# Two hybrid decoder layers: wider spacing in the gate chain, a second output tile, key and query stores and attention one step later

## The chip, the cores and the metric

The kernel runs on one core of one Trainium2 chip. Its engines work side by side, each through its own list of instructions in order: TensorE (PE, matrix products; PEld are its weight loads), VectorE (DVE), ScalarE (ACT), GpSimd (POOL) and SyncE (SP, which issues most of the DMAs). An instruction that needs another engine's result waits on a semaphore, and everything behind it on its engine waits too. The metric is the device time of one execution in microseconds (us), lower is better; the times are medians of a few runs.

## What is computed

Two layers over 1024 positions of width 1024. Each layer has an adaptive norm, one wide projection, four mLSTM heads and four retention heads of width 256, an output projection and a gated residual. Cut to what matters here:

```python
for l in range(2):
    shift, scale, gate = split(silu(c) @ w_ada[l] + b_ada[l], 3)
    h = rmsnorm(x, norm_g[l]) * (1 + scale) + shift
    mq, mk, mv, mo, mz, mi, mf, rq, rk, rv, rz = split_cols(h @ w_in[l])
    mq, mk = split(silu(causal_conv4(concat(mq, mk)) + conv_b))
    cell = mlstm(mq, mk, mv, mi + b_i, mf + b_f)   # exp input gate, sigmoid forget gate, running max
    y_m = sigmoid(mo) * head_norm(cell) * silu(mz)
    ret = retention(rotary(rq), rotary(rk), rv)    # decay 1 - 2^(-5-head)
    y_r = head_norm(ret) * silu(rz)
    x = x + gate * (concat(y_m, y_r) @ w_out[l])
return rmsnorm(x, final_g)
```

The mLSTM needs, per head and position, running sums of the log forget gate and a running maximum of the input gate minus that sum. That small computation on 4 heads x 1024 positions is the *gate chain* below. All matrix products run in pairs of rounded parts (high and low), three products for one (`mm3`, lines 177 to 179).

## The kernel before

**Products.** The projections of a layer are a list of jobs (`plan`): `v45` the values of heads 4 and 5, `z4` the gate path of head 4, `q4` and `k4` its queries and keys, `a..` gate paths of mLSTM heads. Heads 0 to 3 are mLSTM, 4 to 7 retention. In layer 0 the list starts `v45 v67 z4 q4 k4 z5 q5 k5`, in layer 1 `v45 z4 q4 k4 q5 k5 v67`. A job is one level of a seven-product scheme: products a11, S1, S2, a12, S4, S3, a22 over half-size operands, each 12 matmuls of 512 columns, or for values twice 24 matmuls of 256 columns. One such product is a *step*. Products collect in four PSUM banks, px and pz, two of each; ScalarE (L775, L825, L830) and VectorE (L778, L782, L785, L826, L832, L835) move them out to tiles `acc`, a pool of 12. Weights come as tiles R by DMA; ScalarE rounds them to wH (L404) and VectorE or GpSimd makes the low part (L409).

**What sets the order.** TensorE's order is the order of the code. After every step `tick()` runs whatever small generators are due: a generator's `yield n` puts its next part off by n steps. So the number of products between two parts of a generator is the number in its `yield`. On the other engines a list scheduler places the instructions by its own estimate, apart from those marked `late(...)`, which keep the program's order. On VectorE, `Later()` marks whole helpers so (their records all have line L144).

**The gate chain** (`gate_chain`, L502 to L597) is such a generator. Parts: raw gates from PSUM to SBUF on ScalarE; store to DRAM and load back with 32 partitions of 128 positions; log sigmoid on ScalarE; on VectorE the two running sums (`bq`, `br`); then TensorE sums the carries over blocks (L547), VectorE adds them and takes the running maximum; TensorE transposes the block maxima (L556); VectorE scans them; TensorE spreads the result (L561); VectorE finishes; store of the maximum to DRAM (L567); TensorE transposes four tables (L571) and VectorE and ScalarE make the factors for the mLSTM. In layer 0 it runs beside `rotary_tables`, and in both layers beside `build_forms`, which makes half-size sums of the inputs on VectorE (L634 to L655).

**Keys and queries.** `conv_chain` (mLSTM) and `rot_done.chain` (retention) end in `spill`: the tile is stored to DRAM (qdr or kfr, L935), and for keys a VectorE transpose of it (L902) is stored too (kdr, L904). All go through SP's queue.

**Attention** of a head (`attention`) starts 4 steps after its key job has ended and follows `TABLE`, one entry for each step: loads of q, k, v from DRAM (L999, L1013), splits (L876, L928, L929), scores S, values V, state updates U (L1099, L1102, L1104). `values` collects the output of one chunk of 256 positions in a tile: `nd` for mLSTM (one buffer, 258 columns per half with the denominator), `n` for retention (one buffer). `normalise` and `finish` read it later and transpose it (L1192) before the store (L1197). The only other user of `nd` is a rotary table, which holds it from its load (L975, L976) to the last retention key.

The yields of the chain, in order, are

```python
yield 3   # before the load back
yield 3   # before the log sigmoid
yield 2   # before the running sums
yield 3   # before L547
yield 3   # before L556
yield 3   # before L561
```

Of the kernel before, what the change touches and what calls it, by code (L numbers as in the profile page):

```python
# [19 lines left out]
P = 128  # L20
# [67 lines left out]
def tile_hybrid_trunk(ctx, tc, x, xt, c, positions, w_ada, b_ada, norm_g, w_in, w_blk, w_val, conv_w, conv_b,  # L88
# [415 lines left out]
    def gate_chain(l, pgs, gt):  # L504
# [5 lines left out]
        for half in range(2):  # L510
            for r in (0, 32):
                A.activation(raw[r:r + 4, half * HALF:(half + 1) * HALF], pgs[half][r:r + 4, :], AF.Identity,
                             bias=bg[r:r + 4, :])
        for i in range(2):
            Q.dma_start(gtd[l][i], raw[32 * i:32 * i + 4, :])
# [13 lines left out]
        yield 3  # L529
        for i, t in enumerate((fb, li)):  # L530
            Q.dma_start(t, gtd[l][i].rearrange("h (b t) -> (h b) t", t=P))
        yield 3
# [3 lines left out]
        yield 2  # L536
# [7 lines left out]
        yield 3  # L544
# [9 lines left out]
        yield 3  # L554
# [4 lines left out]
        yield 3  # L559
# [319 lines left out]
    def conv_chain(l, hg, which, m, half, pt):  # L879
# [16 lines left out]
        spill(acc, l, hg, which, m, half)  # L896

    def k_store(src, l, hg, m, half):
        zt = wt("acc", 512, NACC)
        n = HALF - half * CH  # L900
        a = n // P
        V.transpose(zt[:, 0:n].rearrange("p (b a c) -> p a b c", a=a, c=32),  # L902
                    src[:, 0:n].rearrange("p (a b c) -> p a b c", a=a, c=32))
        late(Q.dma_start(kdr[l][hg][half][m * P:(m + 1) * P, 0:n], zt[:, 0:n]))  # L904
# [26 lines left out]
    def spill(src, l, hg, which, m, half):  # L931
        dst = (kfr if which else qdr)[l][hg][half].rearrange("(a p) t -> a p t", p=P)
        if which:
            k_store(src, l, hg, m, half)
        late(Q.dma_start(dst[m], src))  # L935
# [16 lines left out]
    def rot_done(l, hg, which, cosT, sinT):  # L952
        got = {}

        def chain(half):
            p0, n1 = got[0, half], got[1, half]
            for m, (one, two, op) in enumerate(((cosT, sinT, ALU.add), (sinT, cosT, ALU.subtract))):
                s, a = wt("acc", 512, NACC), wt("acc", 512, NACC)
                V.tensor_tensor(a, n1, two[half], ALU.mult)
                V.tensor_tensor(s, p0, one[half], ALU.mult)  # L960
                V.tensor_tensor(s, s, a, op)
                yield 1
                spill(s, l, hg, which, m, half)
# [7 lines left out]
    def load_rotary(rot):  # L971
        for which in range(2):
            for i in range(2):
                t = wt("dm", 512, 2) if which == 0 else wt("nd", 516, 1) if i == 0 else bt()
# [10 lines left out]
    def attention(l, hg, gt):  # L985
# [120 lines left out]
        def values(j, tts):  # L1106
            state = st["state"]
            sH, sL = sds[j]
            if tts[0] == 0:
                st["nd"] = wt("nd", 516, 1).rearrange("p (a b) -> p a b", a=2) if ml else None  # L1110
                nrm[j] = st["nd"][:, :, 0:HD] if ml else wt("n", 512, 1).rearrange("p (a b) -> p a b", a=2)
# [358 lines left out]
    for l in range(DEPTH):  # L1470
# [168 lines left out]
        for j, n, part in slots:  # L1639
# [12 lines left out]
            if left[j] == 0 and jobs[j][0] == "k":  # L1652
                launch(attention(l, jobs[j][1][0], gt), 4, 1)
# [67 lines left out]
```

## Time and profile before

| | us |
|---|---|
| median of 3 runs | 2235.43 |
| lowest, highest | 2228.78, 2241.55 |
| profiled execution | 2231.53 |
| its span, first to last instruction | 2229.8 |
| TensorE busy | 2133.3 (96%) |
| VectorE busy | 1779.0 (80%) |
| ScalarE busy | 1144.5 (51%) |
| GpSimd busy | 942.2 (42%) |
| mean granted TensorE clock | 0.991 |

A row of a profile view names line, engine, operation, the tile written and the tile read (`<-`), count, and times. "Idle before, releaser" says what the engine waited for last. PEclk in the table of windows is the share of full clock that TensorE was granted. Matmuls are pipelined: the time of a row is from its start to its modelled end, so the pace of matmuls is read from how many stand in a window.

### The profile page before, as it was taken

The page shows a single profiled execution, that of the slowest core. Times are in us where ns is not written, and L with a number is a line of the kernel's source. Part 1 is how long each engine was busy: PE and PEld are TensorE (multiplying, and loading weights), DVE is VectorE, ACT ScalarE, POOL GpSimd, SP SyncE. Part 2 cuts the span into 40 slices and gives each one's busy share as a digit, 9 for nine tenths or more (in the row PEclk, how much of TensorE's full clock was granted, in tenths as well). Part 3 has the DMA queues.
Part 4 walks back from the last instruction along what each step waited for, and adds up shares of the span by engine and source line. Part 5 has one row for each costly group of instructions (what it writes and reads, how often), then busy time and mean ns, then how long its engine had stood idle before and what let it go on. Part 6 is the DMA issues. An engine that isn't in the chain of part 4 may idle for free.

```text
span 2229.8 us, 35055 instructions
## 1 busy us (share of the span) xinstructions
PE 2133.3 (96%) x11489; PEld 1818.7 (82%) x11489; DVE 1779.0 (80%) x3139; ACT 1144.5 (51%) x2151; POOL 942.2 (42%) x820
## 2 busy tenths in 40 slices
PE   6889999999999999999998999999999899999998
PEld 5688789888988878888777888888987887888887
DVE  6898888999989999874639687788787888978563
ACT  7535345445556656653544434454556555555342
POOL 1433344444454444424466344444434444442313
PEclk9999999999999999999999999999999999999999
DMA  8267678787786667686632866877867677677874
GB/s 290 58 179 214 198 219 258 212 250 210 215 237 184 196 177 208 190 270 221 208 107 68 247 191 189 230 201 221 224 182 194 187 202 194 176 199 247 224 249 119
DMA packets 452836, 448.44 MB, mean 201 GB/s; under 512 B 191314, under 2 KB 310042, under 8 KB 452652
## 3 DMA queue, kind: packets, MB, share of 16 engines
q1 hardware_dynamic: 432924, 410.27, 59.3%
q0 software_dynamic: 19584, 35.66, 10.5%
q8 instruction: 90, 1.47, 0.3%
q14 instruction: 94, 0.77, 0.1%
q10 hardware_dynamic: 144, 0.26, 0.0%
HBM read 322.76 MB, written 123.31 MB: 200 GB/s over the span
## 4 chain that ended last, share of the span: by engine, by line
PE 44%; DVE 27%; DMA 14%; issue 7%; ACT 3%; POOL 2%; SPq 2%; DVEq 0%; POOLq 0%; ACTq 0%
PE px L177 5%; PE px L178 5%; PE px L179 5%; PE pz L178 4%; PE pz L179 4%; PE pz L177 4%; PE pa L177 3%; PE pa L179 3%; PE pa L178 3%; DVE acc L889 3%; DVE R L409 3%; DMA acc<-kfr 2%; DMA R<-in_w_blk_dram 2%; DVE R L713 2%; DMA R<-in_w_val_dram 2%
## 5 line engine op out<-in xcount | busy, mean ns | idle before, releaser
L404 ACT CAST wH<-R 128x512 fp32r<-128x512 f32 x616 | 378.0, 617 | 468.6 <-PE px L178 133.4
L409 POOL TENSOR_TENSOR R<-R,wH 128x512 fp32r<-128x512 f32 x276 | 391.4, 1425 | 483.5 <-ACT wH L404 317.0
L177 PE MATMUL px<-b,wH 128*128 128x512 f32 x912 | 360.7, 395 | 6.4 <-ACT acc L775 5.8
L179 PE MATMUL px<-b,R 128*128 128x512 f32 x912 | 362.1, 397 | 0.0
L178 PE MATMUL px<-b,wH 128*128 128x512 f32 x912 | 360.8, 396 | 0.0
L409 DVE TENSOR_TENSOR R<-R,wH 128x512 fp32r<-128x512 f32 x340 | 261.9, 774 | 97.7 <-ACT wH L404 87.7
L178 PE MATMUL pz<-b,wH 128*128 128x512 f32 x704 | 279.3, 397 | 1.4 <-DVE b L1266 1.4
L179 PE MATMUL pz<-b,R 128*128 128x512 f32 x704 | 280.0, 398 | 0.0
L177 PE MATMUL pz<-b,wH 128*128 128x512 f32 x704 | 279.2, 397 | 0.0
L177 PEld LDWEIGHTS px<-b,wH 128*128 128x128 f32 x912 | 172.2, 189 | 45.4 <-ACT acc L775 7.6
L179 PEld LDWEIGHTS px<-b,R 128*128 128x128 f32 x912 | 171.6, 188 | 40.3
L178 PEld LDWEIGHTS px<-b,wH 128*128 128x128 f32 x912 | 171.9, 188 | 38.6
L177 PE MATMUL px<-wH,b 128*128 128x256 f32 (+1 forms) x576 | 176.9, 307 | 15.9 <-ACT acc L825 5.8
L178 PE MATMUL px<-R,b 128*128 128x256 f32 (+1 forms) x576 | 173.8, 302 | 7.8 <-DVE R L409 7.8
L179 PE MATMUL px<-wH,b 128*128 128x256 f32 (+1 forms) x576 | 174.4, 303 | 0.0
L709 POOL DMA_DIRECT2D R<-in_w_blk_dram x104 | 93.1, 895 | 172.9 <-DMA R<-in_w_blk_dram 61.3
L178 PEld LDWEIGHTS pz<-b,wH 128*128 128x128 f32 x704 | 133.2, 189 | 32.0 <-DVE b L1266 2.3
L179 PEld LDWEIGHTS pz<-b,R 128*128 128x128 f32 x704 | 132.8, 189 | 31.3
L177 PEld LDWEIGHTS pz<-b,wH 128*128 128x128 f32 x704 | 133.2, 189 | 28.5 <-issue 0.2
L877 POOL TENSOR_TENSOR kc<-acc,kc 128x512 fp32r<-128x512 f32 x64 | 88.0, 1375 | 114.2 <-ACT kc L876 109.0
L177 PE MATMUL pz<-wH,b 128*128 128x256 f32 (+1 forms) x448 | 134.1, 299 | 0.3 <-DVE acc L785 0.3
L179 PE MATMUL pz<-wH,b 128*128 128x256 f32 (+1 forms) x448 | 133.8, 299 | 0.0
(345 smaller groups left out, 5282.3 us busy)
## 6 DMA issues: line engine op xcount, KB each, us to landing
R<-in_w_blk_dram SPq DMA_DIRECT2D x276, 256.0 KB
vdr<-acc SPq DMA_DIRECT2D x128, 256.0 KB
ring<-vdr SPq DMA_DIRECT2D x64, 512.0 KB
R<-in_w_out_dram SPq DMA_DIRECT2D x128, 256.0 KB
R<-in_w_blk_dram POOLq DMA_DIRECT2D x104, 256.0 KB, 4.6
R<-in_w_val_dram SPq DMA_DIRECT2D x80, 256.0 KB
gdr<-acc SPq DMA_DIRECT2D x64, 256.0 KB
acc<-in_w_ada_dram SPq DMA_DIRECT2D x64, 256.0 KB
```

Source lines behind the costliest of these rows:

```text
L177: PE.matmul(o, lt[0], rt[0], start=start, stop=False, skip_group_check=more)
L178: PE.matmul(o, lt[0], rt[1], start=False, stop=False, skip_group_check=more)
L179: PE.matmul(o, lt[1], rt[0], start=False, stop=stop, skip_group_check=more)
L404: A.copy(h, r)
L409: eng.tensor_tensor(lo, r, f(h), ALU.subtract)
L709: G.dma_start(raw[n], src, accum_op=ALU.add)
L713: V.tensor_tensor(raw[n], raw[one], raw[two], ALU.add)
L877: eng.tensor_tensor(dst[1], src, f(dst[0]), ALU.subtract)
L889: V.scalar_tensor_tensor(acc[:, e:], pt[:, o + e - d:o + HALF - d], wcol, acc[:, e:], ALU.mult, ALU.add)
```

## The change

Four edits.

1. The gate chain waits longer between its parts: a new `yield 2` between raw gates and their store; then 3, 3, 2, 3, 3, 3 become 4, 4, 3, 6, 5, 5. Its last two yields (2 and 2) stay.
2. `nd` has two buffers, and retention outputs use it too in place of `n`. The rotary table that takes an `nd` keeps one of the two until the last retention key.
3. `spill` becomes a generator: the transpose of a key tile is made as before, the stores to DRAM (kdr, kfr, qdr) are issued one step later.
4. Attention of a head starts 5 steps after its key job instead of 4.

```diff
@@ gate_chain
                              bias=bg[r:r + 4, :])
+        yield 2
         for i in range(2):
             Q.dma_start(gtd[l][i], raw[32 * i:32 * i + 4, :])
...
-        yield 3
+        yield 4
         for i, t in enumerate((fb, li)):
             Q.dma_start(t, gtd[l][i].rearrange("h (b t) -> (h b) t", t=P))
-        yield 3
+        yield 4
         A.activation(e, fb, AF.Abs)
...
-        yield 2
+        yield 3
         V.scalar_tensor_tensor(fb, fb, 0.0, e, ALU.min, ALU.subtract)
...
-        yield 3
+        yield 6
         pc = ps_a()
...
-        yield 3
+        yield 5
         pm = ps_a()
...
-        yield 3
+        yield 5
         pb = ps_a()
@@ conv_chain
-        spill(acc, l, hg, which, m, half)
+        yield from spill(acc, l, hg, which, m, half)
@@ k_store
-        late(Q.dma_start(kdr[l][hg][half][m * P:(m + 1) * P, 0:n], zt[:, 0:n]))
+        return lambda: late(Q.dma_start(kdr[l][hg][half][m * P:(m + 1) * P, 0:n], zt[:, 0:n]))
@@ spill
+        store = k_store(src, l, hg, m, half) if which else None
+        yield 1
         if which:
-            k_store(src, l, hg, m, half)
+            store()
         late(Q.dma_start(dst[m], src))
@@ rot_done
-                spill(s, l, hg, which, m, half)
+                done = spill(s, l, hg, which, m, half)
+                launch(done, next(done))
@@ load_rotary
-                t = wt("dm", 512, 2) if which == 0 else wt("nd", 516, 1) if i == 0 else bt()
+                t = wt("dm", 512, 2) if which == 0 else wt("nd", 516, 2) if i == 0 else bt()
@@ values
-                st["nd"] = wt("nd", 516, 1).rearrange("p (a b) -> p a b", a=2) if ml else None
-                nrm[j] = st["nd"][:, :, 0:HD] if ml else wt("n", 512, 1).rearrange("p (a b) -> p a b", a=2)
+                st["nd"] = wt("nd", 516, 2).rearrange("p (a b) -> p a b", a=2) if ml else None
+                nrm[j] = st["nd"][:, :, 0:HD] if ml else wt("nd", 516, 2)[:, 0:512].rearrange("p (a b) -> p a b", a=2)
@@ the loop over products
-                launch(attention(l, jobs[j][1][0], gt), 4, 1)
+                launch(attention(l, jobs[j][1][0], gt), 5, 1)
```

In the built programs the lines of the changed kernel stand one to four higher than those before.

**The gate chain in layer 1, TensorE.** The carry sums are the two matmuls into a tile `pa` from `q`. Before:

```order
L178 MATMUL pz_13946<-R_13818,b_13584 128x256
L179 MATMUL pz_13946<-wH_13816,b_13585 128x256
L547 MATMUL pa_13973<-q_13547 32x1 x2
L177 MATMUL px_13725<-wH_13907,b_13441 128x256
L178 MATMUL px_13725<-R_13909,b_13441 128x256
```

Now:

```order
L178 MATMUL pz_14229<-b_13575,wH_14124 128x512
L179 MATMUL pz_14229<-b_13574,R_14159 128x512
L548 MATMUL pa_14244<-q_13598 32x1 x2
L177 MATMUL px_14205<-b_13432,wH_14161 128x512
L178 MATMUL px_14205<-b_13433,wH_14161 128x512
```

They have moved from the middle of the value products (256 columns) to behind the first two products of `z4` (512 columns): 144 matmuls of 256 columns and 24 of 512 stand between the old place and the new.

**The same place on VectorE.** The running sums are the SCALAR_TENSOR_TENSOR rows that read `ones`; COPY takes the carries out of `pa`. Before:

```order
L655 SCALAR_TENSOR_TENSOR acc_13895<-acc_13893,acc_13895 128x512
L310 SCALAR_TENSOR_TENSOR acc_13712<-acc_13809,cact,acc_13712 128x512
L144 TENSOR_TENSOR q_13547<-q_13547 32x128
L144 SCALAR_TENSOR_TENSOR q_13547<-ones,q_13547 32x128 x2
L144 TENSOR_SCALAR q_13548<-q_13548 32x128
L144 TENSOR_TENSOR q_13547<-q_13548 32x128
L144 COPY q_13548<-pa_13973 32x2
```

Now, from the second running sum on:

```order
L144 SCALAR_TENSOR_TENSOR q_13598<-ones,q_13598 32x128
L144 TENSOR_SCALAR q_13599<-q_13599 32x128
L144 TENSOR_TENSOR q_13598<-q_13599 32x128
L310 SCALAR_TENSOR_TENSOR acc_13710<-acc_13967,cact,acc_13710 128x512
L310 SCALAR_TENSOR_TENSOR acc_13710<-acc_14044,cact,acc_13710 128x512
L801 SCALAR_TENSOR_TENSOR acc_14080<-px_13723,acc_14079 128x512
L409 TENSOR_TENSOR R_14163<-R_13977,wH_14161 128x512
L836 TENSOR_TENSOR acc_13841<-pz_13905,acc_13841 128x512
L714 TENSOR_TENSOR R_13977<-R_13977,R_14085 128x512
L801 SCALAR_TENSOR_TENSOR acc_14114<-px_13765,acc_14113 128x512
L836 TENSOR_TENSOR acc_13881<-pz_13939,acc_13881 128x512
```

Before, two short rows stood between sums and COPY; now thirteen long ones do, the moves of the last value products out of PSUM among them (COPY is five rows further on).

**ScalarE in layer 0, where the second rotary tables are loaded.** ACT_TABLE_LOAD switches the set of functions; L843 (L844 now) are tanh, L976 (L980 now) sine. Before:

```order
L843 ACT_TABLE_LOAD
L843 ACTIVATE acc_2601<-pz_2586 128x512
L404 CAST wH_2674<-R_2504 128x512
L976 ACT_TABLE_LOAD
L976 ACTIVATE b_2668<-b_2668 128x512
L843 ACT_TABLE_LOAD
L843 ACTIVATE acc_2631<-acc_2574 128x512
L976 ACT_TABLE_LOAD
L976 ACTIVATE dm_2662<-dm_2662 128x512
L404 CAST wH_2697<-R_2611 128x512
L843 ACT_TABLE_LOAD
L843 ACTIVATE acc_2653<-acc_2547 128x512
```

Now:

```order
L844 ACTIVATE acc_2601<-pz_2586 128x512
L404 CAST wH_2674<-R_2481 128x512
L844 ACTIVATE acc_2631<-acc_2574 128x512
L404 CAST wH_2697<-R_2611 128x512
L980 ACT_TABLE_LOAD
L980 ACTIVATE b_2668<-b_2668 128x512
L844 ACT_TABLE_LOAD
L844 ACTIVATE acc_2653<-acc_2524 128x512
L980 ACT_TABLE_LOAD
L980 ACTIVATE dm_2662<-dm_2662 128x512
L404 CAST wH_2723<-R_2481 128x512
L776 COPY acc_2693<-px_2680 128x512
```

Before, five switches stood ahead of the copy of px (L775, one CAST behind the last row shown); now three do, since the exponentials of the chain's end, which share the set of tanh, have moved ahead of this place.

**SP's queue in layer 1, at the key stores of head 5.** L999 (L1003 now) are attention's loads for head 4. Before:

```order
L904 DMA kdr_5_1_214<-acc_15161 128x256
L935 DMA kfr_5_1_278<-acc_15139 128x512
L913 DMA acc_15246<-kdr_4_0_211 32x8x64 x4
L904 DMA kdr_5_1_214<-acc_15219 128x256
L935 DMA kfr_5_1_278<-acc_15165 128x512
L904 DMA kdr_5_0_213<-acc_15223 128x512
L935 DMA kfr_5_0_277<-acc_15170 128x512
L999 DMA acc_15302<-kfr_4_1_276 128x2x256
L999 DMA acc_15304<-qdr_4_1_244 128x2x256
```

Now:

```order
L905 DMA kdr_5_1_214<-acc_15156 128x256
L938 DMA kfr_5_1_278<-acc_15131 128x512
L905 DMA kdr_5_1_214<-acc_15214 128x256
L938 DMA kfr_5_1_278<-acc_15158 128x512
L905 DMA kdr_5_0_213<-acc_15216 128x512
L938 DMA kfr_5_0_277<-acc_15163 128x512
L914 DMA acc_15275<-kdr_4_0_211 32x8x64 x4
L905 DMA kdr_5_0_213<-acc_15255 128x512
L938 DMA kfr_5_0_277<-acc_15218 128x512
L1003 DMA acc_15343<-kfr_4_1_276 128x2x256
L1003 DMA acc_15345<-qdr_4_1_244 128x2x256
```

Three pairs of stores stood ahead of those loads; now all four do.

## Prediction

> **What bounds the kernel now.** I read the head of the page first, for the engine that sets the end.
>
> ```profile
> span 2229.8 us, 35055 instructions
> PE 2133.3 (96%) x11489; PEld 1818.7 (82%) x11489; DVE 1779.0 (80%) x3139; ACT 1144.5 (51%) x2151; POOL 942.2 (42%) x820
> ```
>
> TensorE works for 96% of the span. No edit adds or removes a product, so the time can change only through TensorE's pauses and its clock. The second view is therefore TensorE's waits; its columns are the instruction, the result it waited for, and total, number and longest in us.
>
> ```profile
> PE pa L547 <- DVE q L144: 10.7, 2, 8.1
> ...
> PE pa L177 <- DVE cf L1099: 7.8, 4, 2.4
> PE px L178 <- DVE R L409: 7.8, 3, 5.4
> PE px L177 <- ACT acc L775: 5.8, 4, 2.7
> PE px L177 <- ACT acc L825: 5.8, 3, 3.1
> PE pa L1121 <- POOL sL L1079: 5.8, 5, 2.6
> PE pa L179 <- DVE b L929: 4.8, 7, 1.4
> ...
> PE pa L556 <- DVE q L144: 3.0, 1, 3.0
> ```
>
> The longest wait of the part shown is the gate chain's: the carry sums (L547) wait for VectorE's running sums once in each layer, 8.1 us and 10.7 - 8.1 = 2.6 us. The transpose of block maxima (L556) waits once, 3.0 us. Next I looked at the windows round these three waits, and at some undisturbed ones beside them. The columns are stretch and length, busy time and count of PE, PEld, DVE, ACT and POOL, then PEclk, DMA share and GB/s.
>
> ```profile
> 127.00:137.00 10.00, 7.72 (x52) 7.55 (x52) 9.90 (x22) 1.81 (x4) 2.94 (x3) 0.83 0.26 85
> 143.00:153.00 10.00, 9.51 (x67) 9.47 (x68) 8.49 (x24) 2.36 (x4) 1.75 (x2) 0.83 0.91 242
> 1225.00:1235.00 10.00, 5.39 (x34) 5.29 (x35) 9.90 (x21) 5.16 (x8) 3.86 (x3) 0.66 0.93 269
> 155.00:165.00 10.00, 10.00 (x86) 10.00 (x85) 9.76 (x24) 2.82 (x5) 2.92 (x2) 1.00 1.04 227
> 205.00:215.00 10.00, 10.00 (x44) 8.06 (x43) 8.58 (x16) 3.77 (x6) 3.60 (x3) 1.00 0.58 162
> 125.00:165.00 40.00, 34.08 (x256) 33.17 (x255) 37.20 (x87) 13.24 (x23) 10.45 (x9) 0.91 0.73 199
> 165.00:205.00 40.00, 38.86 (x289) 36.84 (x288) 36.14 (x85) 19.11 (x35) 14.23 (x10) 1.00 0.74 209
> ```
>
> Two things are to be seen. A pause costs more than its length: the granted clock of the first three windows is 0.83, 0.83 and 0.66, where the undisturbed ones have 1.00. And VectorE is full there (9.90 of 10 us in two of them): TensorE waits because VectorE has a queue, not because a result takes long. The fourth and fifth windows give the pace: 86 matmuls of 256 columns or 44 of 512 in 10 us, 0.116 and 0.227 us each. A step is 24 of the first or 12 of the second, so 2.8 or 2.7 us.
>
> **The change, part by part.** The sum is made against the profiled execution's own time, 2231.53 (span 2229.8 plus 1.7 around it). The median of the runs, 2235.43, lies 3.9 above that and the lowest, 2228.78, lies 2.7 below.
>
> *Waits of the gate chain: -13.7.* Ahead of L547 stand 3 more steps than before, 3 x 2.8 = 8.4 us, against waits of 8.1 and 2.6. Ahead of L556 stand 2 more, 5.6 us, against 3.0. That is enough if VectorE doesn't come later itself. The parts before L547 are also put off, by 2 + 1 + 1 + 1 = 5 steps, but in layer 1 VectorE is behind anyway, as its timeline shows (start, duration, operation):
>
> ```profile
> 1228.24 0.74 DVE L310 SCALAR_TENSOR_TENSOR acc<-acc,cact,acc 128x512 f32<-128x512 f32 x1
> ...
> 1229.10 0.72 DVE L144 TENSOR_TENSOR_SCAN q<-ones,q 32x128 f32<-32x128 f32 x2
> ```
>
> The scans end at 1229.8 (1229.10 + 0.72) and the carry sums start with them, so TensorE had come at 1229.8 - 8.1 = 1221.7. In the new order about a dozen more rows, most of the kind of L310, stand ahead of the scans. At 0.7 each they cost some 8.4 us, which puts the sums at about 1238. TensorE now comes 3 + 5 = 8 steps later, 8 x 2.77 = 22 us, so at 1243.9. The slack is about 6 us. In layer 0 TensorE came to L547 at 126.6, as this row shows (start, duration, and in brackets the idle time before it):
>
> ```profile
> 129.18 0.53 PE L547 MATMUL pa<-q 32*32 32x1 f32 x4 [2.62 <-DVE q L144]
> ```
>
> Those 22 us later it now comes at 148.6. With 13 us more of rows ahead of it, an estimate of some 18 rows at 0.7 us, VectorE would be done near 142. So all three waits go: 8.1 + 2.6 + 3.0 = 13.7. The bounds are 0 (the sums slip as far as TensorE's order does) and 13.7.
>
> *The clock behind them: -5.1.* A window of 10 us at 0.83 lost 1.7 us of full clock, which is 3.4 us at half speed. The two windows of layer 0 give 1.7 + 1.7. The one of layer 1 lost 3.4 us at 0.66, but TensorE stood still for 8.1 us in it, so I count half, 1.7. The sum is 5.1, the bounds 0 and 6.8.
>
> The Trainium skill, page "TensorE: Matmul & The Clock Gate", section "What's actually happening", says that the clock falls to half only after at least one idle window of about 3.4 us. By that rule the pauses of 2.6 and 3.0 us would cost no clock, the gain would be 3.4 us smaller, and the sum below would be 3.4 us higher. The trace disagrees: both windows have 0.83.
>
> *VectorE in layer 0 gives part back: +2.3.* Over the 80 us of the last two windows VectorE works 37.20 + 36.14 = 73.34, so it idles 6.7. Layer 0 is to win 2.6 + 3.0 of waits and 3.4 of clock there, 9.0 us. If the same VectorE work must fit in 80 - 9.0 us, 2.3 us are missing and show as new short waits later. The bounds are 0 (the work can spread into what follows) and +9.0 (VectorE stays the bound and nothing is won).
>
> *ScalarE's table loads: -2.3 and +0.6.* At the end of the chain in layer 0 ScalarE switches between exponentials, sines and tanh:
>
> ```profile
> 212.70 1.28 ACT L843 ACT_TABLE_LOAD   x1 [4.52 <-DVE pz L778]
> ...
> 217.06 1.28 ACT L843 ACT_TABLE_LOAD   x1
> 218.36 0.63 ACT L843 ACTIVATE acc<-acc 128x512 f32<-128x512 f32 x1
> ...
> 223.79 0.58 ACT L775 COPY acc<-px 128x512 f32<-128x512 f32 x1
> ```
>
> From 212.7 to the copy of px at 223.79 are 11.1 us, with five loads of 1.28. That copy is what TensorE waits for, the 2.7 of the L775 row. In the new order three loads stand there and eight operations of about 0.62: 3 x 1.28 + 8 x 0.62 = 8.8 us, 2.3 earlier. The bounds are 0 and the 2.7 that there is to win. Elsewhere layer 0 gets four loads more, two in total; these stand ahead of copies that have room, so I take 0.6 of 2 x 1.28 = 2.6 (bounds 0 and 2.6).
>
> The Trainium skill, page "ScalarE: Activation LUTs", section "What ACT_TABLE_LOAD costs", adds about 1.38 us of draining to each load, 2.66 us for a switch. By that the two added loads would cost 5.3 us and speak against the change. The trace has the operation behind the load at 217.06 start 1.30 later, so no draining shows.
>
> *Stores one step later: -2.* SP runs its list in order. Its waits for the transposes that it stores, and ScalarE's for the loads behind them, are these:
>
> ```profile
> SPq L904 <- DVE acc L902: 128.6, 39, 9.4
> ```
>
> ```profile
> ACT kc L876 <- DMA acc<-kfr: 82.6, 41, 5.3
> ...
> ACT n L1150 <- DVE zt L1192: 11.3, 8, 2.9
> ```
>
> One such case of layer 1, SP first and then ScalarE:
>
> ```profile
> 1362.88 0.43 SPq L935 DMA_DIRECT2D kfr<-acc  x1
> ...
> 1364.34 0.46 SPq L999 DMA_DIRECT2D acc<-kfr  x1
> ```
>
> ```profile
> 1369.10 0.62 ACT L876 CAST kc<-acc 128x512 fp32r<-128x512 f32 x1 [5.00 <-DMA acc<-kfr]
> ...
> 1372.17 0.57 ACT L825 COPY acc<-px 128x512 f32<-128x512 f32 x1
> ```
>
> The load of k is issued at 1364.34, ScalarE stands 5.0 us for it, and the copy of px at 1372.17 comes late: TensorE's 3.1 of the L825 row. A store issued a step after its transpose, 2.7 us later, no longer holds SP for that time (3.3 us a wait on average, 128.6 by 39), and loads behind it leave earlier. Against that, the tiles stay taken a step longer in the pool of 12, and in layer 1 all four pairs of stores, not three, stand ahead of attention's loads. The bounds are -5.8 (all of the L825 row) and +2 (one more pair of stores, two issues near 0.43 us, and a pause of clock). I take -2, nearer to the middle, since each of the three waits is of one load only.
>
> *The second `nd`: 0.* ScalarE waits 11.3 us in 8 times for the tile of retention outputs (`n`, L1150 above), but it works only 51% of the span, and none of TensorE's longer waits names that tile. While the rotary table holds one, retention still has one buffer as before.
>
> *Attention one step later: 0.* Its loads get 2.7 us more, but nothing ahead of it is removed. The bounds are -9 and +9, half of the 7.8 + 5.8 + 4.8 us that its products wait (L1099, L1079, L929), as it meets other work either way.
>
> *The end of the chain: +1.* It now falls into copies of the next job (gate paths of head 4 in layer 0, queries in layer 1) and the load of the maximum. The nearest row is this wait of VectorE:
>
> ```profile
> DVE wd L144 <- DMA ME<-mdr: 2.7, 1, 2.7
> ```
>
> Nothing waited for VectorE there. I take 1 of the bounds 0 and 2.7.
>
> The wait for R (L409, 7.8) stays: the work ahead of its long case at 5.4 us comes before the chain's first changed part.
>
> The sum is -13.7 - 5.1 + 2.3 - 2.3 + 0.6 - 2 + 1 = -19.2, so 2231.5 - 19.2 = 2212.3. As the profiled execution lies under the median of the runs, I say 2213.
>
> **The rivals.** *VectorE binds layer 0.* The waits there move to whatever VectorE does next, and SP gains nothing. For it speak 37.20 of 40 us; against it 36.14 in the next 40, and 8.58 of 10 later, so the queue thins out. The sum loses 9.0 - 2.3 = 6.7 and 2: -10.5, about 2221.
>
> *The waits only move, and the change doesn't do what it says.* The running sums are put off by 5 steps, and if VectorE's list puts them behind as much other work, TensorE waits as long, later. For it speaks that VectorE's queue, not the sums, was late; against it the slack of about 6 us above. Without -13.7, -5.1 and +2.3 remain -2.7: about 2229 to 2230.
>
> *Slower: attention falls out of step with the other work.* One step later, the state updates on VectorE (L1099) meet the taps of the next head's convolution, and the products that need them wait. That is one wait in each of 24 updates of the mLSTM heads; 4 of them wait now, 7.8 by 4 = 1.95 us each, with half of a clock loss of 1.7 behind it 2.8. From 19.2 by 2.8 = 7 more waits the change is no gain; from 12 to 13 it is slower than the median by half a per cent. At 14 the time is 2231.5 - 19.2 + 39.2 = 2251. For it speaks that attention's products already wait for L1099, L1079 and L929, in rows of 7.8, 5.8 and 4.8; against it that 20 of the 24 wait for nothing, and VectorE idles a fifth of the span.
>
> **How the numbers follow.** My forecast has a chance of 0.47, its own range 2201 to 2223 (-5.8 for the stores, 2.7 for the table loads and some of attention's -9 below; layer 0's +9.0 above). VectorE as the bound of layer 0 has 0.18, waits that only move 0.15, attention out of step 0.17, and a gain beyond 2198 from attention's waits 0.03. Half a per cent, 11 us, is about what a measurement of this kernel tells from no change: faster is below 2224.3, slower above 2246.6. Faster: 0.47, 0.15 of the 0.18 and 0.03, in all 0.65. Slower: the cases of attention from 13 waits up, 0.12 of the 0.17. The rest, 0.23, is the same. The range of 2198 to 2240 leaves out the 0.03 below and most of the attention cases, about 0.15, above.
>
> **What would show it.** Right: in TensorE's waits the rows of the carry sums and of the transpose of block maxima are gone or under 1 us; the windows from 125 to 165 and at the carry sums of layer 1 have PEclk 1.00; ScalarE's copy of px near 224 no longer ends a wait of 2.7; SP's waits for transposes have fallen well under 128.6; VectorE's share rises with the shorter span. Wrong: these rows stand at another place of the chain (the spread of the maxima, or the four tables) with the same sum; new short waits for VectorE's copies fill layer 0 up to 250 us; the row of the state updates (L1099) has over 10 waits; or the table loads show as waits for ScalarE's copies.

## The result

The changed kernel takes 2251.52 us (median of 13 runs, 2244.89 to 2259.72) against 2234.79 for the kernel before (13 runs, 2226.33 to 2243.82). The ratio is 1.0081, with a 95% interval of 1.0067 to 1.0095: 18 us slower, where the prediction had 2213 and a range of 2198 to 2240. (Ratios are worked out from all runs, so they are not quite those of the medians; gains and losses in us are worked out from the ratios.) Two of the kernels below had one execution each that took far longer than all others (3452 and 8512 us); it is left out of their medians and ratios.

The profiled execution of the changed kernel took 2256.68 us. The head of its page and its clock, and the clock of the kernel before beside it:

```profile
span 2255.0 us, 35103 instructions
...
PE 2145.5 (95%) x11489; PEld 1829.7 (81%) x11489; DVE 1780.5 (79%) x3139; ACT 1151.9 (51%) x2153; POOL 946.0 (42%) x820
```

```profile
core 0: 2255.0 us, clock 0.982
```

```profile
core 0: 2229.8 us, clock 0.991
```

The span grew by 25.2 us, more than the 18 us of all runs: of the two executions profiled, the one before lies 3 us under its kernel's median, the one now 5 us over. TensorE runs the same 11489 matmuls, yet its busy time grew from 2133.3 to 2145.5, 12.2 us, at a mean granted clock of 0.982 instead of 0.991; the other 13.0 us are pauses. How pauses and clock share the loss is not fixed by one pair of traces: the other executions of the kernel before have a clock of 0.983 to 0.990, those of the changed kernel 0.979 to 0.985.

TensorE's waits in the changed kernel (lines are one to four higher):

```profile
PE pa L179 <- DVE b L930: 21.1, 8, 6.2
PE px L177 <- DVE acc L833: 12.4, 3, 5.5
PE pa L1125 <- POOL sL L1083: 10.9, 6, 3.9
...
PE px L177 <- DVE acc L962: 8.1, 2, 4.2
PE px L178 <- DVE R L409: 7.8, 3, 5.4
...
PE pa L1125 <- ACT sH L1082: 4.3, 4, 1.6
...
PE px L177 <- ACT acc L776: 0.9, 1, 0.9
```

The rows of the gate chain, 10.7 and 3.0, are gone, and the wait for ScalarE's copy (L776) fell from 5.8 to 0.9. In their place TensorE waits for VectorE's copy of px (L833, 12.4; as L832 it was 1.4 before) and, above all, attention's products wait. The low parts of the split keys (L930, before L929) went from 4.8 to 21.1; the state's parts on GpSimd and ScalarE (L1083, L1082) take 10.9 and 4.3, where they took 5.8 and 0.4.

These are the windows round the two longest waits for L833 and round the longest wait for L930 (columns as in the prediction):

```profile
129.00:139.00 10.00, 4.96 (x33) 4.79 (x32) 9.72 (x23) 4.45 (x9) 2.58 (x3) 0.82 0.64 211
...
1239.00:1249.00 10.00, 4.50 (x30) 4.32 (x29) 7.35 (x10) 5.52 (x9) 4.45 (x3) 0.78 0.95 270
...
413.00:423.00 10.00, 7.62 (x32) 6.48 (x33) 7.65 (x17) 1.62 (x3) 0.88 (x1) 0.72 0.81 221
```

The two stretches that were to be freed still have pauses and PEclk under 1, and there is a new one in the middle of attention. What happened there is seen on VectorE. Its timeline and TensorE's next one, in the changed kernel (start, duration):

```profile
407.59 0.68 DVE L409 TENSOR_TENSOR R<-R,wH 128x512 fp32r<-128x512 f32 x1
408.19 0.69 DVE L962 TENSOR_TENSOR acc<-acc,b 128x512 f32<-128x512 f32 x1
...
410.12 1.75 DVE L310 SCALAR_TENSOR_TENSOR acc<-acc,cact,acc 128x512 f32<-128x512 f32 x1
...
414.27 0.70 DVE L1196 STREAM_TRANSPOSE zt<-nd 128x512 f32<-128x512 f32 x1
414.89 0.83 DVE L930 SCALAR_TENSOR_TENSOR b<-acc,kc,b 128x256 fp32r<-128x256 f32 x2
```

```profile
415.38 0.58 PE L179 MATMUL pa<-ring,b 128*128 128x256 f32 x1 [6.24 <-DVE b L930]
```

The same place in the kernel before:

```profile
400.91 0.70 DVE L1192 STREAM_TRANSPOSE zt<-n 128x512 f32<-128x512 f32 x1
401.54 1.28 DVE L929 SCALAR_TENSOR_TENSOR b<-acc,kc,b 128x256 fp32r<-128x256 f32 x2
...
405.15 0.68 DVE L959 TENSOR_TENSOR acc<-acc,b 128x512 f32<-128x512 f32 x1
```

Before, transpose and split stood ahead of the rotary rows (L959); now, a step later, they stand behind them (L962 is that line in the changed kernel) and behind rows of L310. TensorE needs the split and stands 6.24 us. This is one place only; whether it is the cause was the main question of the experiments.

### The profile page after: what moved, and what is told of

Same layout as the page of the kernel before. It is cut to its first block, busy times and chain, and to the rows that moved or that the text cites. A ratio compares the mean times of both kernels' runs of the same rounds, so it can differ in the third digit from the quotient of the medians.

```text
span 2255.0 us, 35103 instructions
## 1 busy us (share of the span) xinstructions
PE 2145.5 (95%) x11489; PEld 1829.7 (81%) x11489; DVE 1780.5 (79%) x3139; ACT 1151.9 (51%) x2153; POOL 946.0 (42%) x820
## 5 line engine op out<-in xcount | busy, mean ns | idle before, releaser
L404 ACT CAST wH<-R 128x512 fp32r<-128x512 f32 x616 | 379.5, 619 | 495.5 <-PE px L178 157.8
L409 DVE TENSOR_TENSOR R<-R,wH 128x512 fp32r<-128x512 f32 x340 | 269.4, 796 | 108.5 <-ACT wH L404 97.9
L177 PE MATMUL px<-wH,b 128*128 128x256 f32 (+1 forms) x576 | 178.2, 309 | 25.8 <-DVE acc L833 12.4
L177 PEld LDWEIGHTS px<-wH,b 128*128 128x128 f32 x576 | 116.6, 202 | 30.0 <-issue 16.2
L177 PE MATMUL pz<-wH,b 128*128 128x256 f32 (+1 forms) x448 | 134.8, 301 | 0.4 <-DVE acc L890 0.4
```

The costliest lines, as they stand in the source:

```text
L177: PE.matmul(o, lt[0], rt[0], start=start, stop=False, skip_group_check=more)
L404: A.copy(h, r)
L409: eng.tensor_tensor(lo, r, f(h), ALU.subtract)
```

## The experiments

Each ratio is to the kernel before on the same chip, with its 95% interval; 0.001 is 2.2 us.

### One edit at a time

**The gate chain alone.**

```diff
         (before the store of the raw gates)
+        yield 2
-        yield 3 / 3 / 2 / 3 / 3 / 3
+        yield 4 / 4 / 3 / 6 / 5 / 5
```

> Only the seven yields of the gate chain are changed. Theory (the chain's own waits go, but TensorE then meets VectorE's queue a few steps later, and attention a step later is what costs): the pauses of the two stretches fall from 10.5 to about 8.3 us in layer 0 and from 8.2 to 5.7 in layer 1, as in the trace of the whole change, so 4 to 5 us faster: about 2230, ratio 0.998. Rival 1 (the prediction's sum holds for this edit alone, and another edit spoils it): 14 to 19 us faster, about 2218, ratio 0.992, without a wait for the copies of px (L833). Rival 2 (the spacing itself costs): slower than 2235.

2223.85 us, ratio 0.9955 (0.9936 to 0.9973): 10 us faster, between theory and first rival. The chain's waits are gone, and this row of TensorE's waits has grown, shown first as it was before:

```profile
PE px L177 <- DVE acc L832: 1.4, 2, 1.1
```

```profile
PE px L177 <- DVE acc L833: 12.9, 4, 5.2
```

On VectorE in layer 1 that copy stands at the end of a queue:

```profile
1221.14 1.78 DVE L310 SCALAR_TENSOR_TENSOR acc<-acc,cact,acc 128x512 f32<-128x512 f32 x1
1223.64 0.95 DVE L310 SCALAR_TENSOR_TENSOR acc<-acc,cact,acc 128x512 f32<-128x512 f32 x1 [0.73 <-DMA acc<-in_w_ada_dram]
1224.51 1.75 DVE L409 TENSOR_TENSOR R<-R,wH 128x512 fp32r<-128x512 f32 x1
1226.19 1.27 DVE L833 TENSOR_TENSOR acc<-px,acc 128x512 f32<-128x512 f32 x2
```

TensorE no longer waits at the carry sums; it runs on to the product that needs px back, and there meets the same busy VectorE. So the whole change's waits for L833 come from this edit, and most of the pause moved instead of going away: in the windows 125 to 165, 165 to 205 and 1215 to 1255 together TensorE's idle time is 11.4 us, where it was 15.2.

**The second `nd` alone.**

```diff
-    wt("nd", 516, 1) ... wt("n", 512, 1)
+    wt("nd", 516, 2) ... wt("nd", 516, 2)[:, 0:512]
```

> Only the second buffer of nd, shared with the retention outputs, is changed. Theory: no change beyond 5 us, ratio 0.998 to 1.002, since TensorE's order is the same. Rival (the shared tile makes retention outputs wait for the rotary table or for the other heads): 10 to 18 us slower, ratio 1.005 to 1.008, with longer waits of ScalarE for nd and of TensorE for pa.

2231.40 us, ratio 0.9994 (0.9979 to 1.0010): nothing, as the theory had it.

**Attention one step later alone.**

```diff
-                launch(attention(l, jobs[j][1][0], gt), 4, 1)
+                launch(attention(l, jobs[j][1][0], gt), 5, 1)
```

> Only attention's start is changed, 5 steps after the key job instead of 4. Theory: this is what costs: 20 to 25 us slower, about 2257, ratio 1.009 to 1.011, with TensorE's waits for the low part of the score operands (L929 here) near 20 us against 4.8, and half-speed stretches spread over the attention parts. Rival (the stores or the second nd cost, not the start): within 5 us of the kernel before.

2250.89 us, ratio 1.0088 (1.0067 to 1.0108): 19.6 us slower, which is more than the whole change loses. Two of its waits:

```profile
PE pa L179 <- DVE b L929: 20.9, 9, 5.8
PE pa L547 <- DVE q L144: 11.0, 2, 8.1
```

The gate chain's wait is as before, and the wait for the key splits is there in full. The span of this profile is 2248.4, 18.6 longer; TensorE's busy time is 2141.6, 8.3 longer at a clock of 0.984 against 0.991, and 10.3 are pauses. These shares are of one pair of traces: the second `nd`, which costs nothing and leaves TensorE's order as it was, has 2140.6 of busy time in its profile, at 0.986. That the clock is lower does hold over the runs: 0.980 to 0.984 in the six of this kernel, 0.985 to 0.990 in the twenty of the kernel before beside them.

One part of the price is a row on ScalarE. At the end of layer 0 it loads the sine's table (L976) and then needs tanh again (L852). Before:

```profile
948.62 0.59 ACT L852 ACTIVATE acc<-px 128x512 f32<-128x512 f32 x1
949.23 1.28 ACT L976 ACT_TABLE_LOAD   x1
```

With attention at 5 steps:

```profile
958.78 1.28 ACT L976 ACT_TABLE_LOAD   x1
...
961.86 1.28 ACT L852 ACT_TABLE_LOAD   x1
963.15 0.60 ACT L852 ACTIVATE acc<-px 128x512 f32<-128x512 f32 x1
```

```profile
PE px L177 <- ACT acc L852: 4.6, 1, 4.6
```

The row that empties px now stands behind two loads, and TensorE waits 4.6 us for it, where it waited 0.6. In every kernel here with attention at 5 steps in layer 0 that wait is 3.0 to 4.6; at 6 steps it is 2.3, at 11 0.2. So this is some 2 to 4 us of the price, as the traces have it; no run takes the loads away alone.

**Attention and the stores.**

```diff
     def spill(src, l, hg, which, m, half):
+        store = k_store(src, l, hg, m, half) if which else None
+        yield 1
         if which:
-            k_store(src, l, hg, m, half)
+            store()
```

> Attention 5 steps after the key job, and the key and query stores one step after their transposes (the stores alone can't be moved: with attention at 4 steps a load would come ahead of its store). Theory: within 4 us of the kernel with attention's start alone. Rival 1 (later stores relieve SP, as predicted): 2 to 6 us faster than that kernel. Rival 2 (later stores hold their tiles and the loads longer): 5 us or more slower than that kernel.

2258.37 us, ratio 1.0124 (1.0101 to 1.0147), 0.0036 above attention alone. The other way round, the whole change with only the stores put back:

> The whole change but for the stores, which are issued at once again. Theory (the later stores cost a little, as the fourth kernel was 7 us slower than the third): about 2245, ratio 1.004 to 1.006, against 1.008 of the whole. Rival (they cost nothing, the difference was that of two runs): 1.007 to 1.009.

2243.61 us, ratio 1.0062 (1.0047 to 1.0077), 0.0019 below the whole. Both pairs point to a cost of later stores, of 4 to 8 us, though the intervals of each pair overlap; neither shows a gain. SP's wait for the transposes that it stores (L904 for L902) went from 126.2 us to 115.5 in the first pair, and is 123.4 in the whole change against 128.6 before.

**The gate chain and `nd` together,** that is the whole change without its two later starts:

> The whole change without its two later starts: the gate chain's yields and the two buffers of nd, with attention at 4 steps and stores at once. Theory (the edits add up): 0.9955 x 0.9994 = 0.995, 2218 to 2223. Rival (with the chain's rows gone from their place, the second buffer costs or gains by itself): outside 0.993 to 0.9975.

2223.34 us, ratio 0.9966 (0.9951 to 0.9980). The edits add up within their intervals: -10.0 for the chain, -1.3 for `nd`, +19.6 for attention and +4 to +8 for the stores make +12 to +16; the whole has +18 (15 to 21).

### What holds the gate chain's gain down

**The adaptive rows out of the way in layer 1.**

```diff
-        launch(adaptive(l, gcol, gb), 2 if l else 30)
+        launch(adaptive(l, gcol, gb), 10 if l else 30)
```

> The gate chain's yields alone, and in layer 1 the adaptive rows of the gate (adaptive, L308 and L310 on VectorE) launched after 10 steps instead of 2. Theory (with the chain spaced out, TensorE waits for the copy of px at L833 because VectorE works through a queue, in layer 1 with L308 and L310 in it, 0.48 + 1.78 + 0.95 = 3.2 us): that wait in layer 1 falls from 5.0 to about 2 us, 2 to 5 us faster than the gate chain alone, ratio to before 0.993 to 0.9945. Rival 1 (VectorE's other rows fill the place, or the copy waits for something else): the wait stays over 4 us, ratio 0.9955. Rival 2 (the rows cost as much where they go): 0.9955 or above with the wait gone.

2222.57 us, ratio 0.9970 (0.9952 to 0.9988), not told apart from the chain alone. The wait in layer 1 is 4.5 us where it was 4.9. Without L308 and L310 VectorE filled the place with other rows (L635 and L656, which are L634 and L655 before), and then stood idle for a row ahead of the copy:

```profile
1226.57 1.50 DVE L409 TENSOR_TENSOR R<-R,wH 128x512 fp32r<-128x512 f32 x1 [2.26 <-ACT wH L404]
1228.00 1.27 DVE L833 TENSOR_TENSOR acc<-px,acc 128x512 f32<-128x512 f32 x2
```

It waits 2.26 us for ScalarE's cast (L404), with the copy behind that row in its list. First rival.

**The sums not put off.**

```diff
         (gate chain: only the last three of these yields changed)
-        yield 3 / 3 / 2 / 3 / 3 / 3
+        yield 3 / 3 / 2 / 6 / 5 / 5
```

> The gate chain with only its last three yields changed (6, 5, 5); the store, load, log sigmoid and running sums stay where they were. Theory (TensorE stands to VectorE's queue, whichever row of it is waited for): the gain of the chain's edit stays as it is, ratio 0.994 to 0.997, with waits of some 5 us left in the two stretches. Rival 1 (putting the sums off pushed VectorE's work onto the copies at L832): the waits there are under 2 us and the ratio is 0.990 to 0.993. Rival 2 (the later sums are needed, since they keep ScalarE and SP apart): 0.998 or above.

2226.04 us, ratio 0.9977 (0.9961 to 0.9992): a gain of 5 us, between theory and second rival; its interval touches that of the whole chain. The copies (L832 here) wait 13.1 us in all, 6.7 at the longest. Which row of VectorE's queue TensorE is made to wait for changes little.

**One more weight part on GpSimd.**

```diff
-    POOL_LOW = ("S1", "S3", "a22")
+    POOL_LOW = ("S1", "S3", "a22", "a12")
```

> The gate chain's yields alone, with the low parts of one more of the seven products' weights (a12) made by GpSimd instead of VectorE: 0.8 us less of VectorE for each such row of L409, 1.46 us more of GpSimd. Theory (VectorE's queue is what bounds the freed stretches and half of TensorE's pauses): faster than the gate chain alone, ratio 0.989 to 0.9945. Rival (GpSimd becomes late with the weights, or its rows slow VectorE's): 0.996 or above, with new waits of TensorE for R or sL.

2252.27 us, ratio 1.0087 (1.0065 to 1.0109): the rival, and 29 us worse than the chain alone. The engines' row of its page:

```profile
PE 2145.6 (95%) x11489; PEld 1827.6 (81%) x11489; DVE 1800.7 (80%) x3071; ACT 1146.9 (51%) x2151; POOL 1039.9 (46%) x888
```

68 rows left VectorE, and yet its busy time rose from 1779.7 (the chain alone) to 1800.7; with the full number of rows the other kernels' profiles that compute the same have 1773.0 to 1790.5. The mean row went from 1779.7 / 3139 = 0.57 us to 1800.7 / 3071 = 0.59. Of the rival, the part that is seen is the one of VectorE's rows: TensorE's waits for R are 8.3 us against 7.4 and for sL 7.4 against 4.6. What grew more are waits for the state updates and for the state's parts on ScalarE (L1100 from 5.6 to 10.3, L1079 from 0.6 to 6.9).

### Why a later attention costs

**The key splits alone back at their old step.**

```diff
-    "Q0 K0 m0 d1", "s0 k1", ... "U01", "s1 d2 K2", ... "V11 U3 k3", "s2 q3"
+    "Q0 K0 m0 d1 s0", "k1", ... "U01 s1", "d2 K2", ... "V11 U3 k3 s2", "q3"
```

> Attention 5 steps after the key job, and in its table of steps the splits of the transposed keys (entries s0, s1, s2, the rows of L928 and L929) one step earlier, so that they fall on the old step while the rest of attention stays late. Theory (the splits' low part on VectorE, now queued behind the rotary or convolution rows of the next product, is the main cost): TensorE's wait for L929 falls from 20.9 to under 7 us, and 8 to 15 us of the 19.5 come back: 2236 to 2243, ratio 1.002 to 1.005. Rival 1 (the whole of attention meets other work, and this row is only where it shows): the wait moves to other rows and the ratio stays at 1.007 or above. Rival 2 (the splits stand in the way of other rows when early): above 1.0088.

2257.34 us, ratio 1.0127 (1.0104 to 1.0150): above all that the theory allowed. The wait for L929 is gone from TensorE's waits, and others took its place:

```profile
PE pa L177 <- DVE cf L1099: 7.5, 4, 2.9
PE px L177 <- DVE acc L959: 7.0, 3, 3.2
PE px L177 <- DVE acc L782: 6.8, 3, 2.6
PE px L177 <- DVE acc L889: 6.7, 2, 3.4
```

So that theory fell: the price doesn't hang on that row alone. Whether it was only where the loss showed (first rival) or the early splits cost as much elsewhere (second rival, which also allows this ratio) is not told apart.

**The chains of queries and keys one step later too,** so that attention stands to them as at 4 steps:

```diff
-                launch(chain(half), 1 - half)
+                launch(chain(half), 2 - half)
-            launch(conv_chain(l, hg, which, m, half, src), delay)
+            launch(conv_chain(l, hg, which, m, half, src), delay + 1)
```

> Attention 5 steps after the key job, and the convolution and rotary chains of queries and keys launched one step later too, so that attention stands to them as it did at 4, while TensorE's order stays that of the third kernel, instruction for instruction. Theory (attention's VectorE rows lost their place beside the chains' rows, L889 and L959 to L961): most of the cost comes back, ratio 1.000 to 1.004, TensorE's wait for L929 under 8 us. Rival (what counts is where attention stands against the products themselves and their copies, which this leaves at 5): 1.007 to 1.013.

2267.59 us, ratio 1.0167 (1.0142 to 1.0193), worse still, with these waits:

```profile
PE px L177 <- DVE acc L959: 12.1, 4, 4.4
PE pa L179 <- DVE b L929: 12.0, 5, 6.4
PE pa L1121 <- POOL sL L1079: 10.9, 6, 2.4
```

So giving attention its old place beside those chains does not bring the time back either.

**Six and eleven steps.**

```diff
-                launch(attention(l, jobs[j][1][0], gt), 4, 1)
+                launch(attention(l, jobs[j][1][0], gt), 6, 1)      (and 11)
```

> Attention 6 steps after the key job. Theory A (each place has its own collisions, 4 being a good one): anywhere from 1.000 to 1.012, with another set of rows leading TensorE's waits than at 5. Theory B (later is worse in itself, in proportion): above the 1.009 of 5 steps, near 1.010, and 11 steps at 1.014 would be the same line.

> Attention 11 steps after the key job, which is one whole job of 7 products later than 4. Theory (the price of 5 is one of phase: attention's rows against the rows that end a product of the same job pattern): between 250 us and the layer's last products the pauses and half-speed stretches are like those at 4 steps, with TensorE's wait for L929 under 10 us; what it costs is at the end of each layer, where no products are left beside the last head. Rival (later is worse in itself, by loads, buffers and tiles held): the wait for L929 is 20 us or more and the pauses before the layer's end exceed those at 5 steps.

6 steps: 2253.50 us, ratio 1.0098 (1.0073 to 1.0122). 11 steps: 2262.14 us, 1.0138 (1.0119 to 1.0157). With 1.0088 at 5, the first step costs 0.009, and the six from 5 to 11 together 0.005. From 5 on that is close to a line, some 0.0008 a step, as theory B had it; the step from 4 to 5 is ten times that. At 6 the key splits lead TensorE's waits again (13.3). At 11 another row leads, and the splits wait 8.4, under the 10 that the phase theory asked for:

```profile
PE pa L1121 <- ACT sH L1078: 9.0, 4, 3.8
...
PE pa L179 <- DVE b L929: 8.4, 7, 3.1
```

But the stretches between the layers' ends are not like those at 4 steps. Before, and then at 11:

```profile
250.00:900.00 650.00, 630.83 (x3496) 544.21 (x3495) 591.24 (x1044) 347.34 (x680) 298.63 (x269) 0.99 0.76 213
1340.00:1950.00 610.00, 586.59 (x3422) 514.86 (x3421) 507.70 (x935) 329.67 (x642) 271.80 (x254) 0.99 0.73 201
```

```profile
250.00:900.00 650.00, 626.60 (x3425) 539.47 (x3424) 572.47 (x1008) 334.31 (x649) 289.95 (x260) 0.98 0.74 209
1340.00:1950.00 610.00, 579.94 (x3326) 508.67 (x3326) 495.36 (x883) 315.32 (x610) 267.14 (x241) 0.97 0.70 195
```

TensorE is idle for 23.4 and 30.1 us in them at 11 steps, against 19.2 and 23.4 before, and the clock is lower. So a price of phase against a job of 7 products does not fit either.

**One layer at a time.**

```diff
-                launch(attention(l, jobs[j][1][0], gt), 4, 1)
+                launch(attention(l, jobs[j][1][0], gt), 4 if l else 5, 1)      (and 5 if l else 4)
```

> Attention 5 steps after the key job in layer 0 alone. Theory (VectorE is 90% busy in that layer's attention, and any shift of its order shows on TensorE): 13 to 19 us slower, ratio 1.006 to 1.0085, most of 1.0088. Rival (the price is the same for every head): 1.003 to 1.0055.

> Attention 5 steps after the key job in layer 1 alone. Theory (VectorE has room there, 82% busy): within 4 us, ratio 0.998 to 1.002. Rival (the same price for every head): 1.003 to 1.0055.

Layer 0: 2245.46 us, ratio 1.0069 (1.0047 to 1.0091). Layer 1: 2238.20 us, 1.0031 (1.0018 to 1.0043). Both cost, and layer 0 about twice as much, as the theory had it for layer 0; that layer 1 costs too is the rival. 0.0069 + 0.0031 agrees with the 0.0088 of both.

**VectorE relieved.** The kernel before and the one with 5 steps, both without the sums of the adaptive rows:

```diff
             if k == 0:
                 late(V.tensor_scalar(acc, raw, cact[:, 0:1], None, ALU.mult))
-            else:
-                late(V.scalar_tensor_tensor(acc, raw, cact[:, k:k + 1], acc, ALU.mult, ALU.add))
```

> Attention at 4 steps; the sums of the adaptive rows on VectorE (L310) are left out, so that the adaptive norm and gates are computed from an eighth of their inputs; loads and the rest stay. In layer 0's attention that is 36 rows and 38.1 us of VectorE less, some 85% busy instead of 90%. Theory (VectorE's load sets TensorE's pauses there): 5 to 15 us faster than before, ratio 0.993 to 0.998. Rival (the load doesn't matter, only single places in the order): 0.998 to 1.002.

> The same rows left out, with attention at 5 steps. Theory (VectorE's load sets the price of the later start): the distance to the kernel of the same call at 4 steps shrinks from 19.5 to under 10 us, 0.0045 of the ratio. Rival (the price is of single places in the order and stays when VectorE has room): 15 to 25 us, 0.0065 to 0.011.

2221.79 us, ratio 0.9951 (0.9932 to 0.9970), and 2242.64 us, ratio 1.0050 (1.0032 to 1.0069). Taking 50 us of busy time off VectorE (1728.9 against 1779.0) gave 11 us, so its load does matter to TensorE. But the distance between 4 and 5 steps stayed at 0.0099, 22 us. A load lower by that much does not lower the price of the later start: the theory of this pair fell too.

**The later heads one step earlier.**

```diff
-    RELEASE = 22
+    RELEASE = 21
```

> Attention at 4 steps after the key job, but a head frees the next one after 21 entries of its table instead of 22 (RELEASE), so that the heads whose key job ends while another's attention runs start one step earlier. Theory A (lateness costs: less cover behind the start): 0.996 to 1.001. Theory B (TensorE's order before is one that fits, and any other arrangement of attention among the products costs by scattered pauses): slower, ratio 1.003 to 1.010, with TensorE's waits of attention's products (pa) up and half-speed stretches added.

In this kernel the heads overlap by one entry more, and some of what it computes comes out otherwise. 2276.20 us, ratio 1.0191 (1.0162 to 1.0220). It can't decide between the two theories, for a wait of a new kind leads:

```profile
PE pa L177 <- DMA ring<-vdr: 28.6, 14, 6.2
```

TensorE waits for the loads of values (vdr), which it did not before; that row alone is over half of the 43 us.

## Why the prediction was wrong

The step that failed is the one that read *"Attention one step later: 0"*, with bounds of -9 and +9. It measures +19.6 us alone, and with that size there the sum of -19.2 is +0.4 instead: no gain is left. Most of the rest of the way to +18 is the chain, which gains some 7 us less than its terms, and the stores, 6 to 10 us worse than theirs. Two things were wrong in the step. Its bounds came from the waits that attention's products had before, 4.8 for L929 among them; a shift of all of attention against all other work made new ones (L929 20.9, and L852 on ScalarE 4.6), so the present ones bound nothing. And it priced no clock, while the later start lowers it in every run (0.980 to 0.984 against 0.985 to 0.990).

The rival *"attention falls out of step with the other work"*, with a chance of 0.17, was right in kind and wrong in the rows. It looked for the waits at the state updates (L1099); these fell (7.8 before, 1.6 us at 5 steps), and the key splits and the rotary rows (L959, 6.4) led instead. Its 2251 for 14 such waits agrees with the measured time by luck: in the changed kernel TensorE waits for none. The state's parts on GpSimd, 10.9 in the whole change, are no sign of it: they wait 5.0 with attention alone at 5 steps and 11.6 with the second `nd` alone, which costs nothing.

*Waits of the gate chain, -13.7, and the clock behind them, -5.1:* the waits went, the gain did not follow. The chain's terms added up to -17.2 (with the table loads, what layer 0 gives back and the chain's end); alone it measures -10.0, with 6 to 14 in the interval. The slack for the carry sums held (in the chain alone they start at 1245.8 in layer 1, and the second running sum ends at 1234.2); what the step left out is who asks VectorE next. The copy of px (L833) did, and TensorE waits some 5 us for it in both layers. The term for layer 0, +2.3, was meant for this, and there was none for layer 1, where VectorE's queue held as well. The clock term failed with it: in the changed kernel the windows with those pauses have 0.82 and 0.78. It also rested on one trace. With attention alone at 5 steps, the chain's yields as before, the pause of 2.5 us at the block maxima is followed by full clock (1.00 from 141 to 151).

*Table loads, -2.3 and +0.6:* the first is right; the wait for the copy near 224 is 0.9 where L775 had 2.7, with the chain alone too. The second is too small. The two added loads come from the later attention, not from the chain (ScalarE has 2153 instructions with attention alone at 5, 2151 before and with the chain alone), and they don't stand ahead of rows that have room: TensorE waits for L853 behind one of them, 3.0 us in the changed kernel, where it waited 0.6 for the same row before.

*Stores, -2:* no such gain is seen; two pairs of runs give +4 to +8, with overlapping intervals. The step that SP no longer stands for the transposes failed, for that wait is 123.4 where it was 128.6. TensorE's wait for ScalarE's copy that was to go (L825, 5.8) did go, to 0.5, but it is 0.5 with attention alone too, so the stores didn't take it away. What later stores cost instead was not followed to a row.

*The second `nd`, 0:* right.

What stays open is why 4 steps is so much better than 5, 6 and 11 (an earlier start, as 3, was not run). The table loads are some 2 to 4 us of it. Not one of these alone explains the rest: the key splits' place, the place against the chains of queries and keys, a price in proportion to the delay, the phase against a job, and 50 us of VectorE's load. The traces at 5 steps in both layers do not show more waits but longer ones: between 250 and 2060 us TensorE waits 39 times and 65.6 us with attention alone at 5, against 43 times and 55.8 us before, and no one row has them all. That the old order simply avoids more of these than another would, without one cause, fits the runs but was not shown.

## What to carry over

When a change moves a long procedure as a whole against the others, the waits it has now say little about those it will get: try that edit alone first. A wait on a full engine that is removed at one instruction can come back at the next that needs that engine, as here, so look for who that is and take the difference of the two as the gain. Here the best of the kernels that compute the same is the chain's edit alone, 0.9955 of the time before (0.9936 to 0.9973) and 28 us under the whole change; with `nd` added, or with the adaptive rows moved, it is not told apart from that.

## What the runs showed of the hardware

Moving 68 rows of 128x512 from VectorE to GpSimd made VectorE busier, not less busy. In the trace of the chain alone, VectorE has 1144 tensor-tensor rows of that size. Of the 735 that ran while GpSimd computed nothing, none took over 1 us, and their mean is 0.68. Of the 409 that overlapped a GpSimd operation, 126 took over 1 us, up to 4.65, and their mean is 0.98. All 126 read both inputs from SBUF; of the 252 rows that read one from PSUM 119 overlapped too, and none took over 1 us. With one more part on GpSimd 464 rows overlapped and 150 took over 1 us. The rows that stay thus pay for the rows that moved. The Trainium skill, page "SBUF — State Buffer", section "SBUF: two separate sides", says that the two engines take turns on a shared port, for a whole instruction at a time, where VectorE reads two inputs from SBUF and GpSimd's operation reads SBUF as well; the long rows agree with that.

With the same matmuls, TensorE's busy time differed by up to 20 us between kernels (2130.8 for the gate chain alone, 2151.3 with attention at 11 steps), with the mean granted clock at 0.990 and 0.980. A short pause can be paid for a second time in the clock, but need not be. These are two windows of the kernel before, with one pause each, of 2.4 us for a state update (L1099) and of 2.7 us for the copy near 224 (L775):

```profile
787.00:797.00 10.00, 8.13 (x33) 6.96 (x34) 9.13 (x17) 3.87 (x7) 1.27 (x1) 0.83 0.52 164
222.00:232.00 10.00, 7.58 (x33) 6.13 (x34) 6.46 (x9) 6.11 (x11) 4.65 (x4) 1.00 0.83 250
```

The first has 0.83, the second, with the longer pause, 1.00. So the prediction's *"A pause costs more than its length"* holds for the windows that it chose and not for every one.
